# Seven products of a weight pair in another order: the high weights of two products, then their low ones

## The chip, the cores and the metric

The kernel runs on one core of a Trainium2 chip. The metric is device time in microseconds (us) of one execution, the median of several runs.

## The reference

One layer of a streaming encoder over 512 tokens and 2048 channels, all in float32. A normalised input is multiplied by one wide projection matrix, whose outputs are queries, keys, values and gates of two mixers (sparse attention and a retention recurrence) and two merge gates. The mixers' outputs are projected back, gated, added and sent through `w_o`; a gated side input and a last normalisation follow. Cut to the products, which are nearly all of the work:

```
h = rmsnorm(x)
proj = h @ w_in                      # 2048 x 13392: aq ak av az iq ik iw rq rk rv rz ga gb
a_out = dsa_mixer(aq, ak, av, iq, ik, iw) * silu(az)
b_out = retention_mixer(rope(rq), rope(rk), rv) * silu(rz)
merged = sigmoid(ga) * (a_out @ w_a_out) + sigmoid(gb) * (b_out @ w_b_out)
r = x + merged @ w_o
y = r + (p @ w_ple) * sigmoid(r @ w_ple_gate)
return rmsnorm(y) * final_gain
```

## The kernel before

**Two parts a number.** A float32 operand is split into a high part, rounded to what TensorE's fast float32 form keeps, and a low part, the rest. A product is high by high, high by low and low by high. For weights the high part `wh` is an ACT copy (L137) and the low part `wl` is a DVE subtraction (L142), each of a block of 8 tiles of 128x128, called a unit.

**Pairs.** 48 times, two column blocks of 128 outputs each are computed together by `gemm_pair` (L214): 40 pairs of `w_in` (24 in the retention and gate section, then 4, 8 and 4) and 8 of `w_o`. A pair replaces eight half-sized block products by seven, on sums and differences of the weight blocks and of the activation blocks (named in `PRODUCTS`). So a pair has seven units of weights and seven products, numbered 0 to 6. Each product accumulates into one of four PSUM banks: `banks = (v, p, q, r, p, v, p)`. An activation tile holds its high part in columns 0 to 255 and its low part in columns 256 to 511. So a product is 8 matmuls of the high weights over all 512 columns and 8 of the low weights over the first 256: 112 matmuls a pair, all on L259.

**The order within a pair.** Product by product, 0 to 6; the high weights come first and the low ones second, except in products 4 and 6, where the low weights come first. In this text 0h is the group of eight matmuls with the high weights of product 0, 0l that with its low ones. The order is 0h 0l 1h 1l 2h 2l 3h 3l 4l 4h 5h 5l 6l 6h. After products 0, 1, 4 and 6, ACT copies a bank to SBUF (`pv`, `e1`, `e2`, `e3`, L225); after products 2, 5 and 6, DVE combines banks and copies to outputs (`out`, L227 to L230, then the caller's `done`, such as L887). In the first pair of `w_o` (`late`) the products 0 and 1 run on the first seven tiles and then on the eighth, because the last activations come late.

**Requests.** The emission of instructions is one Python program; the engines run apart, each in the order of its own instructions, held by semaphores. `split_to(n)` (L122) emits the splits of all units below n: at once the ACT copy (L137), and one step later the function `rest`, which holds DVE's subtraction (L142). A step is two matmuls (L262). Where the unit's raw weights are then to become a sum, `rest` also adds another raw tile on DVE (L144) or starts a DMA on the POOL queue that adds a block from HBM into the tile (L105). At the start of product n `split_to` asks for the unit three further (`AHEAD`), and `load_to` (L107) emits the loads on the SP queue for units eight further (L116). There are three buffers each for `wh` and `wl` (`W_BUFS`), and seven for raw tiles (`RAW_BUFS`): a split waits until the matmuls three units back have read the buffer, and a load waits until a raw tile is free. Within a pair, unit 5's ACT copy reads the tile that the DVE addition behind unit 4 (L144) has made.

**Other work in between.** `step` also emits what is due from `later` and from background lists: retention (L743), the top-k rounds and the bias tables. In the retention section the two gate pairs behind each of the eight heads' pairs carry extra matmuls and DVE work.

Of the kernel before, what the change touches and what calls it, by code (L numbers as in the profile page):

```python
# [35 lines left out]
def block_kernel(tc, xT, pT, posb, posq, w_in, w_v, w_ik, w_a, w_b, w_o, w_ple, w_gate,  # L36
                 w_gt, w_pt, fgb, tab, gains, cst, dec, out, out_a, out_b):
    nc = tc.nc
    pe, dve, act, pool, sp = nc.tensor, nc.vector, nc.scalar, nc.gpsimd, nc.sync

    with contextlib.ExitStack() as ctx:
# [10 lines left out]
        def U(name, dt=F32):  # L52
            return up.tile([128, L], dt, name=name, tag="u")
# [4 lines left out]
        def P(name):  # L58
            return pp.tile([128, L], F32, name=name, tag="p")
# [10 lines left out]
        loaded = {}  # L70
# [29 lines left out]
        def view(t, nk, cols):  # L100
            return t.rearrange("p a c -> p (a c)")[:, 0:nk * cols].rearrange("p (a c) -> p a c", c=cols)

        def add_block(r, b):
            src, k0 = b
            pool.dma_start(out=raw_tiles[r], in_=src[:, k0:k0 + 8, :], accum_op=OP.add)  # L105

        def load_to(n):  # L107
            need = max((u[0] for u in units[:n]), default=-1) + 1
            while state["raw"] < need:
                i = state["raw"]  # L110
                src, k0, nk, cols, plus = raws[i]
                if nk * cols <= L and i < 4:
                    t = U("wraw4").rearrange("p (a c) -> p a c", c=128)
                else:
                    t = wp.tile([128, 8, 128], F32, name="wraw", tag="wraw", bufs=RAW_BUFS)
                sp.dma_start(view(t, nk, cols), src[:, k0:k0 + nk, :])  # L116
                raw_tiles[i] = t
                if plus is not None:
                    add_block(i, plus)
                state["raw"] += 1  # L120

        def split_to(n):  # L122
            while state["split"] < min(n, len(units)):
                i = state["split"]
                load_to(i + 1)
                r, plus, nk, cols = units[i]
                if r in unfinished:
                    unfinished[r]()
                raw = view(raw_tiles[r], nk, cols)
                if i in in_raws:  # L130
                    t = wp.tile([128, 2, 512], F32R, name="whl", tag="wraw", bufs=RAW_BUFS)
                    h, l = t[:, 0:1], t[:, 1:2]
                elif nk * cols == L:
                    h, l = (U(n, F32R).rearrange("p (a c) -> p a c", c=cols) for n in ("wh4", "wl4"))
                else:
                    h, l = (view(wp.tile([128, 8, 128], F32R, name=n, tag=n), nk, cols) for n in ("wh", "wl"))
                act.activation(h, raw, AF.Copy)  # L137

                def rest(r=r, plus=plus, l=l, raw=raw, h=h):
                    if unfinished.pop(r, None) is None:  # L140
                        return
                    dve.tensor_sub(l, raw, h.bitcast(F32))  # L142
                    if isinstance(plus, int):
                        dve.tensor_add(raw, raw, view(raw_tiles[plus], nk, cols))  # L144
                    elif plus is not None:
                        add_block(r, plus)

                unfinished[r] = rest
                later(1, rest)
                loaded[i] = (h, l)  # L150
                state["split"] += 1

# [6 lines left out]
        def later(n, f):  # L159
            if n <= 0:  # L160
                return f()
            tick[1] += 1
            heapq.heappush(soon, (tick[0] + n, tick[1], f))

        def step():
            tick[0] += 1
            while soon and soon[0][0] <= tick[0]:
                heapq.heappop(soon)[2]()
            f = todo.popleft() if todo else None
            if f is not None:  # L170
                f()
            elif bg and tick[0] % state["rate"] == 0:
                bg.popleft()()
# [31 lines left out]
        ALL = slice(0, L)  # L205
# [4 lines left out]

        LO, HI = slice(0, 256), slice(256, 512)
        PRODUCTS = ("s3", "a11", "a12", "s4", "s2", "a22", "s1")

        def gemm_pair(ids, X, done, late=False):  # L214

            p, v, q, r = (P("ps_" + n) for n in ("p", "v", "q", "r"))  # L220
            E = {}

            def copy(n, src):
                E[n] = U(n)
                act.activation(E[n], src, AF.Copy)  # L225

            def out(f, x, y, i, c):  # L227
                t = U("e_t")
                f(t, x, y)
                done(t[:, LO], t[:, HI], i, c)  # L230

            def last():
                copy("e3", p)
                out(dve.tensor_sub, p, E["pv"], 1, HI)
                out(dve.tensor_add, r, E["e3"], 1, LO)

            after = {
                0: lambda: copy("pv", v),
                1: lambda: copy("e1", p),
                2: lambda: out(dve.tensor_sub, q, E["e1"], 0, LO),  # L240
                4: lambda: copy("e2", p),
                5: lambda: out(dve.tensor_sub, v, E["e2"], 0, HI),
                6: last,
            }
            banks = (v, p, q, r, p, v, p)
            runs = [(n, range(8), True) for n in range(7)]
            if late:
                runs[0:2] = [(n, range(7), False) for n in (0, 1)] + [(n, (7,), True) for n in (0, 1)]
            count = 0
            for n, ks, end in runs:  # L250
                i, o = ids[n], banks[n]
                if ks[0] == 0:
                    split_to(i + AHEAD - (late and n == 1))
                    load_to(i + AHEAD + LOADS)
                parts = (1, 0) if n in (4, 6) else (0, 1)
                for part in parts:
                    w, c = loaded[i][part], (ALL, LO)[part]
                    for k in ks:
                        pe.matmul(o[:, c], w[:, k], X[PRODUCTS[n]][k][:, c], start=(n < 4 and part == 0 and k == 0),  # L259
                                  stop=(part == parts[1] and k == 7), skip_group_check=True)  # L260
                        count += 1
                        if count % 2 == 0:  # L262
                            step()
                if end and n in after:
                    after[n]()

        def combos(lo, hi, name, keep=None):


            X = {n: [None] * 8 for n in PRODUCTS}  # L270
            T = {}
# [138 lines left out]

        x_split(0)
        split_to(1)
        step()
        x_split(1)
# [254 lines left out]
        hd = dp.tile([56, 128, L], F32, name="hd")  # L669
        x_at = {(n, k): hd[8 * i + k] for i, n in enumerate(PRODUCTS) for k in range(8)}  # L670
        xn = {}
# [10 lines left out]
        _, h_step = combos(lambda k: xn[k], lambda k: xn[k + 8], "h", lambda n, k: x_at[n, k])  # L682
# [168 lines left out]

        Xh = {n: [None] * 8 for n in PRODUCTS}
        x_wanted = collections.deque((n, k) for n in PRODUCTS for k in range(8))

# [25 lines left out]
        def gate_pair(ids, finish):  # L880
            t = B("go")
            outs = [t[:, 0:512], t[:, 512:1024]]
            have = [0, 0]

            def done(c0, c1, i, q):
                o = outs[i]
                dve.tensor_add(o[:, q], c0, c1)  # L887
                have[i] += 1
                if have[i] == 2:
                    later(1, lambda: finish(i, o))  # L890

            gemm_pair(ids, Xh, done)
# [196 lines left out]
        for m in PAIRED:  # L1089
            t = B("sm")  # L1090
            s, o = t[:, 0:512], t[:, 512:1024]
# [17 lines left out]
        for m in range(8):  # L1109
# [9 lines left out]
            def done(c0, c1, i, q, xc=xc):  # L1119
                dve.tensor_add(xc[i][:, q], xc[i][:, q], c0)  # L1120
                dve.tensor_add(xc[i][:, q], xc[i][:, q], c1)
# [14 lines left out]
        for m in range(MF):  # L1136
            i = u_p[m // 4][0]
# [5 lines left out]
            for k in range(2):  # L1143
                a, b = pparts[k]
                w = 2 * (m % 4) + k
# [129 lines left out]
        for i in range(2):  # L1275
            c = (slice(0, 384), slice(384, 512))[i]
# [16 lines left out]
        for q in range(MF // 4):  # L1293
            o = U("yo")
# [6 lines left out]
            o = o.rearrange("p (a c) -> p a c", a=4)  # L1301
# [9 lines left out]
AHEAD = 3  # L1311
LOADS = 5
# [101 lines left out]
```

## Time and profile before

| what | value |
|---|---|
| median of 3 runs | 1686.25 us (1686.04 to 1686.39) |
| profiled execution | 1686.46 us |
| its span, first to last instruction | 1684.7 us |
| granted TensorE clock | 0.998 |
| DVE busy | 1275.3 us (76%) |
| ACT busy | 863.0 us (51%) |
| DMA moved | 355.85 MB, mean 211 GB/s |

The share of busy time on TensorE (PE) counts overlapping matmuls once, and a matmul's end is modelled. So the time that a matmul takes of PE is read here from start to start: in the timeline, consecutive matmuls of one group are one row, and a row's start minus the start before it is what the group before took. In the timeline's rows the first number is the start in us from the span's start, the second the time to the end of the last instruction, then engine, line, operation, output and inputs, shapes and count; a bracket gives idle time before it and what ended it.

### The profile page before, as it was taken

Reading aid. Unit: us, or ns where it says so; the run is one execution under the profiler, and the core shown is the slowest. Engines: PE = TensorE matmul, PEld = TensorE weight load, DVE = VectorE, ACT = ScalarE, POOL = GpSimd, SP = SyncE. Lnnn points to the kernel's source line nnn. Section 1 sums busy time; section 2 is a strip of 40 time slices with the busy share of each in tenths; the row PEclk is TensorE's granted clock in tenths of the full one; section 3 lists DMA queues with packets and bytes.
Section 4 is the critical chain, followed back from the end, with each engine's and each line's share of the span. In section 5 each row is a group of like instructions: output and inputs, shape, how many; then the busy total and the mean of one; then the engine's idle time right before and its main releaser. Section 6 shows DMA issues by size and latency. Waiting matters only on the chain.

```text
span 1684.7 us, 24747 instructions
## 1 busy us (share of the span) xinstructions
PE 1672.4 (99%) x9208; PEld 1451.1 (86%) x9208; DVE 1275.3 (76%) x2020; ACT 863.0 (51%) x1278; POOL 214.8 (13%) x216
## 2 busy tenths in 40 slices
PE   9999999999999999999999999999999999999997
PEld 7988888888888888888888888888888888888897
DVE  7797888987878878877876876787768877864453
ACT  7465423555555555555554555566644444463342
POOL 2100000111111111111331111100000111112222
PEclk9999999999999999999999999999999999999999
DMA  7438989788788788788988889898566788733222
GB/s 288 126 107 310 374 298 327 182 229 220 183 219 213 200 215 212 198 213 215 250 237 214 217 206 233 246 368 278 177 200 189 193 229 214 204 116 100 88 63 100
DMA packets 135369, 355.85 MB, mean 211 GB/s; under 512 B 14801, under 2 KB 26961, under 8 KB 135249
## 3 DMA queue, kind: packets, MB, share of 16 engines
q1 hardware_dynamic: 102496, 256.20, 44.3%
q0 software_dynamic: 21376, 77.60, 25.5%
q10 hardware_dynamic: 11376, 20.47, 3.3%
q8 instruction: 72, 1.18, 0.3%
q14 instruction: 49, 0.39, 0.1%
HBM read 301.26 MB, written 52.95 MB: 210 GB/s over the span
## 4 chain that ended last, share of the span: by engine, by line
PE 94%; DVE 2%; ACT 1%; DMA 1%; issue 1%; POOL 0%; SPq 0%; POOLq 0%; ACTq 0%; DVEq 0%
PE ps_p L259 23%; PE ps_v L259 16%; PE ps_r L259 8%; PE ps_q L259 8%; PE ps_vn L726 3%; PE ps_vn L727 3%; PE ps_vn L728 3%; PE ps_w L198 3%; PE ps_w L197 3%; PE ps_w L199 3%; PE ps_pg L199 3%; PE ps_pg L197 3%; PE ps_pg L198 3%; PE ps_iq L197 1%; PE ps_iq L199 1%; PE ps_iq L198 1%
## 5 line engine op out<-in xcount | busy, mean ns | idle before, releaser
L142 DVE TENSOR_TENSOR wl<-wraw,wh 128x1024 fp32r<-128x1024 f32 (+2 forms) x459 | 562.1, 1232 | 201.7 <-ACT wh L137 198.4
L137 ACT ACTIVATE wh<-wraw 128x1024 fp32r<-128x1024 f32 (+2 forms) x459 | 474.1, 1042 | 283.5 <-DVE wraw L144 129.3
L105 POOL DMA_DIRECT2D wraw<-w_in x120 | 106.3, 960 | 837.6 <-DVE wl L142 264.3
L225 ACT ACTIVATE e<-ps_p 128x512 f32<-128x512 f32 x144 | 86.1, 598 | 158.6 <-PE ps_p L259 151.5
L259 PE MATMUL ps_p<-hs,wh 128*128 128x512 f32 x640 | 161.3, 394 | 0.0
L259 PEld LDWEIGHTS ps_p<-hs,wh 128*128 128x128 f32 x640 | 114.9, 189 | 21.2 <-issue 0.7
L726 PE MATMUL ps_vn<-wh,hh 128*128 128x512 f32 x256 | 99.8, 390 | 0.0
L727 PE MATMUL ps_vn<-wl,hh 128*128 128x512 f32 x256 | 99.7, 390 | 0.0
L728 PE MATMUL ps_vn<-wh,hl 128*128 128x512 f32 x256 | 99.7, 389 | 0.0
L259 PE MATMUL ps_p<-hs,wl 128*128 128x256 f32 x640 | 92.0, 284 | 0.7 <-DVE wl L142 0.7
L259 PEld LDWEIGHTS ps_p<-hs,wl 128*128 128x128 f32 x640 | 83.0, 192 | 1.4 <-DVE wl L142 0.9
L259 PE MATMUL ps_r<-hs,wh 128*128 128x512 f32 x320 | 82.2, 395 | 0.0
L259 PE MATMUL ps_v<-ha,wh 128*128 128x512 f32 x320 | 80.6, 393 | 0.0
L259 PE MATMUL ps_p<-ha,wh 128*128 128x512 f32 x320 | 80.4, 393 | 0.0
L259 PE MATMUL ps_q<-ha,wh 128*128 128x512 f32 x320 | 80.1, 392 | 0.0
L259 PE MATMUL ps_v<-hs,wh 128*128 128x512 f32 x320 | 79.6, 390 | 0.1
L199 PE MATMUL ps_pg<-rh,wl 128*128 128x512 f32 x192 | 74.8, 390 | 0.0
L197 PE MATMUL ps_pg<-rh,wh 128*128 128x512 f32 x192 | 74.7, 389 | 0.0
L198 PE MATMUL ps_pg<-rl,wh 128*128 128x512 f32 x192 | 74.7, 389 | 0.0
L887 DVE TENSOR_TENSOR go<-e_t 128x256 f32<-128x256 f32 x160 | 68.1, 425 | 5.6
L259 PEld LDWEIGHTS ps_v<-hs,wh 128*128 128x128 f32 x320 | 59.8, 188 | 13.2 <-ACT wh L137 0.5
L259 PEld LDWEIGHTS ps_v<-ha,wh 128*128 128x128 f32 x320 | 59.3, 188 | 12.5 <-issue 0.5
(361 smaller groups left out, 3499.4 us busy)
## 6 DMA issues: line engine op xcount, KB each, us to landing
wraw<-w_in SPq DMA_DIRECT2D x172, 512.0 KB, 5.5
wraw<-w_in POOLq DMA_DIRECT2D x120, 512.0 KB, 8.4
wraw<-w_v SPq DMA_DIRECT2D x32, 512.0 KB, 5.0
wraw<-w_o SPq DMA_DIRECT2D x32, 512.0 KB, 5.1
wraw<-w_o POOLq DMA_DIRECT2D x24, 512.0 KB, 6.7
wraw<-w_gate SPq DMA_DIRECT2D x24, 512.0 KB, 4.1
hd<-hs SPq DMA_DIRECT2D x32, 256.0 KB, 5.2
hs<-hd SPq DMA_DIRECT2D x32, 256.0 KB, 5.4
```

The lines of the kernel that those rows point to most:

```text
L105: pool.dma_start(out=raw_tiles[r], in_=src[:, k0:k0 + 8, :], accum_op=OP.add)
L137: act.activation(h, raw, AF.Copy)
L142: dve.tensor_sub(l, raw, h.bitcast(F32))
L197: pe.matmul(o, h[:, k, w], a, start=(s == order[0]), stop=False)
L198: pe.matmul(o, h[:, k, w], b, start=False, stop=False)
L199: pe.matmul(o, l[:, k, w], a, start=False, stop=(s == order[-1]))
L225: act.activation(E[n], src, AF.Copy)
L259: pe.matmul(o[:, c], w[:, k], X[PRODUCTS[n]][k][:, c], start=(n < 4 and part == 0 and k == 0), stop=(part == parts[1] and k == 7), skip_gr ...
L726: pe.matmul(pss[t], a[:, tok(t)], h[:, k], start=(s == 0), stop=False)
L727: pe.matmul(pss[t], a[:, tok(t)], l[:, k], start=False, stop=False)
L728: pe.matmul(pss[t], b[:, tok(t)], h[:, k], start=False, stop=(s == KT - 1))
L887: dve.tensor_add(o[:, q], c0, c1)
```

## The change

The order of the fourteen groups of a pair becomes 0h 1h 0l 1l 2h 3h 2l 3l 4l 4h 5h 5l 6l 6h: the first four products in twos. From 4l on nothing is moved. In the late pair the first four groups run on seven tiles and then on the eighth.

The requests are moved with it. `SPLIT_AT` gives, by place in the new order, up to which unit is asked for. Unit 3 is now asked for at 0l (place 2), before the copy `pv` rather than behind it, and its DVE subtraction is emitted five steps later instead of one, so that it stands behind 0l, whose buffer of low weights it overwrites. Unit 5 is asked for at 3l (place 7), behind 2l, instead of at 3h. In the late pair unit 3 is asked for at 1l instead. All other units are asked for after as many matmuls as before. Loads are asked for at every second place. SP's order of instructions is the same as before. DVE's combination after product 2 stands behind 2l, now one group later.

```diff
-        def split_to(n):
+        def split_to(n, lag=1):
...
-                later(1, rest)
+                later(lag, rest)
...
+        RUNS = [(n, part) for part, ns in enumerate(((0, 1), (0, 1), (2, 3), (2, 3, 4), (4, 5), (5, 6), (6,)))
+                for n in ns]
+        RUNS = [(n, part % 2) for n, part in RUNS]
+
+        SPLIT_AT = {0: 3, 2: 4, 3: 4, 4: 5, 7: 6, 8: 7, 10: 8, 12: 9}
+        LOAD_AT = (0, 2, 4, 6, 8, 10, 12)
...
-            runs = [(n, range(8), True) for n in range(7)]
+            runs = [(n, part, range(8)) for n, part in RUNS]
             if late:
-                runs[0:2] = [(n, range(7), False) for n in (0, 1)] + [(n, (7,), True) for n in (0, 1)]
+                runs[0:4] = [(n, part, ks) for ks in (range(7), (7,)) for n, part, _ in runs[0:4]]
+            ended = [0] * 7
             count = 0
-            for n, ks, end in runs:
+            for at, (n, part, ks) in enumerate(runs):
+                at = max(at - 4, 0) if late else at
                 i, o = ids[n], banks[n]
-                if ks[0] == 0:
-                    split_to(i + AHEAD - (late and n == 1))
-                    load_to(i + AHEAD + LOADS)
-                parts = (1, 0) if n in (4, 6) else (0, 1)
-                for part in parts:
-                    w, c = loaded[i][part], (ALL, LO)[part]
-                    for k in ks:
-                        pe.matmul(o[:, c], w[:, k], X[PRODUCTS[n]][k][:, c], start=(n < 4 and part == 0 and k == 0),
-                                  stop=(part == parts[1] and k == 7), skip_group_check=True)
-                        count += 1
-                        if count % 2 == 0:
-                            step()
-                if end and n in after:
+                if at in SPLIT_AT and not (late and at == 2):
+                    split_to(ids[0] + SPLIT_AT[at], 5 if at == 2 else 1)
+                if at in LOAD_AT:
+                    load_to(ids[LOAD_AT.index(at)] + AHEAD + LOADS)
+                w, c = loaded[i][part], (ALL, LO)[part]
+                first = ended[n] == 0
+                for k in ks:
+                    ended[n] += 1
+                    pe.matmul(o[:, c], w[:, k], X[PRODUCTS[n]][k][:, c], start=(n < 4 and first and k == 0),
+                              stop=(ended[n] == 16), skip_group_check=True)
+                    count += 1
+                    if count % 2 == 0:
+                        step()
+                if ended[n] == 16 and n in after:
                     after[n]()
```

## The prediction

> **What bounds the kernel now.** I read the page first: span, busy times, and the chain that ended last.
>
> ```profile
> span 1684.7 us, 24747 instructions
> ...
> PE 1672.4 (99%) x9208; PEld 1451.1 (86%) x9208; DVE 1275.3 (76%) x2020; ACT 863.0 (51%) x1278; POOL 214.8 (13%) x216
> ...
> PE 94%; DVE 2%; ACT 1%; DMA 1%; issue 1%; POOL 0%; SPq 0%; POOLq 0%; ACTq 0%; DVEq 0%
> ```
>
> PE is never free: 99% busy, 94% of the chain. DVE and ACT matter only where a split comes after the matmul that wants it. Next, PE's own waits, the whole of what the waits view has for L259:
>
> ```profile
> PE ps_p L259 <- DVE wl L142: 0.7, 1, 0.7
> ```
>
> One wait over 0.15 us in 5376 matmuls. So no waiting worth the name is there to be removed; what the change can give must come out of the matmuls' own pace. For that I read the timeline of one undisturbed pair (the second of the four az pairs), PE alone:
>
> ```profile
> 1046.78 1.98 PE L259 MATMUL ps_v<-hs,wh 128*128 128x512 f32 x8
> 1048.59 1.12 PE L259 MATMUL ps_v<-hs,wl 128*128 128x256 f32 x8
> 1049.54 2.00 PE L259 MATMUL ps_p<-ha,wh 128*128 128x512 f32 x8
> 1051.38 1.12 PE L259 MATMUL ps_p<-ha,wl 128*128 128x256 f32 x8
> 1052.34 2.00 PE L259 MATMUL ps_q<-ha,wh 128*128 128x512 f32 x8
> 1054.18 1.11 PE L259 MATMUL ps_q<-ha,wl 128*128 128x256 f32 x8
> 1055.13 2.00 PE L259 MATMUL ps_r<-hs,wh 128*128 128x512 f32 x8
> 1056.97 1.11 PE L259 MATMUL ps_r<-hs,wl 128*128 128x256 f32 x8
> 1057.92 1.12 PE L259 MATMUL ps_p<-hs,wl 128*128 128x256 f32 x8
> 1058.88 2.00 PE L259 MATMUL ps_p<-hs,wh 128*128 128x512 f32 x8
> 1060.72 1.98 PE L259 MATMUL ps_v<-ha,wh 128*128 128x512 f32 x8
> 1062.54 1.11 PE L259 MATMUL ps_v<-ha,wl 128*128 128x256 f32 x8
> 1063.49 1.12 PE L259 MATMUL ps_p<-hs,wl 128*128 128x256 f32 x8
> 1064.45 2.00 PE L259 MATMUL ps_p<-hs,wh 128*128 128x512 f32 x8
> 1066.29 0.39 PE L259 MATMUL ps_v<-hs,wh 128*128 128x512 f32 x1
> ```
>
> Differences of starts give what each group takes. High groups (wh) behind a low one: 1h 1051.38 - 1049.54 = 1.84, and 2h, 3h, 4h, 6h also 1.84. High groups behind a high one: 0h 1.81, 5h 1.82, so 1.815. Low groups (wl) behind a high one: 0.95, 0.96, 0.95, 0.95, 0.95, mean 0.952; behind a low one (4l, 6l) 0.96. A step from low to high thus costs a high group 0.025 us, and a step from high to low saves a low group 0.008: a net 0.017 us for each time the pair goes down and up again. The pair takes 19.51.
>
> **The change part by part.**
>
> *The order of the groups.* Before, a pair steps from low to high at 1h, 2h, 3h, 4h and 6h. After, 1h stands behind 0h and 3h behind 2h; 1l stands behind 0l and 3l behind 2l. Nothing is added or removed: 112 matmuls either way. So two high groups fall from 1.84 to 1.815 and two low ones rise from 0.952 to 0.96: 2 x 0.025 - 2 x 0.008 = 0.034 us a pair, in 48 pairs 1.6 us. Rounding of the starts leaves the 1.6 open by some 0.3 either way. Runs of sixteen are in the rows above (6h and the next 0h, 4h 5h; 3l 4l, 5l 6l); the new runs of twenty-four (6h 0h 1h; 2l 3l 4l) are not, and I take them at the rates of the second eight. Bounds: nothing (if the 0.025 were the price of something that stays), and 48 x 2 x 0.025 = 2.4 if the low groups did not rise. I take the 1.6.
>
> The Trainium skill ("TensorE: Matmul & The Clock Gate", Back-to-back issue gap) has another rule: a warm matmul takes its column count divided by 2.4 GHz plus about 2.5 ns of its own, so eight would take 1.73 us at 512 columns and 0.87 at 256, whatever stands before them. By it the order of groups saves nothing; the rows above (1.84 against 1.815) do not agree, as far as one pair shows.
>
> *The requests.* What must be in time after the change? From the group times, the new order has, from the start of the pair: 1h at 1.81, 0l 3.63, 1l 4.58, 2h 5.54, 3h 7.38, 2l 9.20, 3l 10.15, 4l 11.11, 4h 12.07, 5h 13.91, 5l 15.72, 6l 16.68. From 4l on that is 0.03 earlier than before. In the same pair, ACT and then DVE:
>
> ```profile
> 1050.89 0.60 ACT L225 ACTIVATE pv<-ps_v 128x512 f32<-128x512 f32 x1 [0.40 <-ACT go L896]
> 1051.39 1.05 ACT L137 ACTIVATE wh<-wraw 128x1024 fp32r<-128x1024 f32 x1
> 1052.54 0.60 ACT L225 ACTIVATE e<-ps_p 128x512 f32<-128x512 f32 x1
> 1053.03 1.06 ACT L137 ACTIVATE wh<-wraw 128x1024 fp32r<-128x1024 f32 x1
> 1056.69 2.01 ACT L137 ACTIVATE wh<-wraw 128x1024 fp32r<-128x1024 f32 x2 [2.61 <-DVE wraw L144]
> ```
> ```profile
> 1052.47 1.23 DVE L142 TENSOR_TENSOR wl<-wraw,wh 128x1024 fp32r<-128x1024 f32 x1 [1.51 <-ACT wh L137]
> 1054.12 1.22 DVE L142 TENSOR_TENSOR wl<-wraw,wh 128x1024 fp32r<-128x1024 f32 x1 [0.42 <-ACT wh L137]
> 1055.38 1.22 DVE L144 TENSOR_TENSOR wraw<-wraw 128x1024 f32<-128x1024 f32 x1
> 1056.52 0.68 DVE L229 TENSOR_TENSOR e_t<-ps_q,e 128x512 f32<-128x512 f32 x1
> 1057.24 0.43 DVE L887 TENSOR_TENSOR go<-e_t 128x256 f32<-128x256 f32 x1
> 1057.79 2.36 DVE L142 TENSOR_TENSOR wl<-wraw,wh 128x1024 fp32r<-128x1024 f32 x2
> ```
>
> Unit 3's high copy (1051.39, that is 4.61 into the pair) stood behind `pv`, which stood behind the caller's `go`. Now it goes ahead of `pv`, into its place behind `go` (1050.89, that is 4.11), and ends at 5.2. It is wanted at 7.38, which was 8.35: 2.2 us to spare, where there were 2.7. Its low part starts at 5.2 instead of 5.69 and is wanted at 10.15: more to spare. `pv` now needs 0l, over at 4.58, and runs about 5.2 to 5.8; `e1` 5.76 as before; unit 4's copy 6.25 as before, and with it DVE's L142 and L144, over at 1056.60 (9.82). So unit 4 pays nothing. Then DVE's combination of bank q (L229, L887) must wait for 2l: over at 10.15 plus about 0.2, by which `e1` follows 1l. It runs 10.35 to 11.5 instead of 9.74 to 10.89, and behind it in DVE's queue the low parts of units 5 and 6 slip by 0.6, from 11.01 to 13.37 to about 11.6 to 14.0. They are wanted at 15.72 and 16.68: 2.9 and 2.7 us to spare. Loads wait for those subtractions to free raw tiles, so they start 0.6 later; a unit's load leads its split by most of a pair, and that hides it. The first weights of the next pair keep their times, but its 1h is wanted 0.95 earlier.
>
> So an undisturbed pair stalls nowhere. The price falls where a copy was already late, on 3h above all. One pair (the fourth of the qk pairs) shows it:
>
> ```profile
> 928.20 2.11 PE L259 MATMUL ps_v<-hs,wh 128*128 128x512 f32 x8
> 930.14 1.11 PE L259 MATMUL ps_v<-hs,wl 128*128 128x256 f32 x8
> ```
> ```profile
> 934.61 0.33 ACTq L924 DMA_DIRECT2D kd<-go  x1
> 934.98 0.60 ACT L225 ACTIVATE pv<-ps_v 128x512 f32<-128x512 f32 x1 [1.70 <-DVE go L887]
> 935.47 1.05 ACT L137 ACTIVATE wh<-wraw 128x1024 fp32r<-128x1024 f32 x1
> ```
>
> Its 0h took 1.94, 0.13 over. 3h will be wanted at 928.20 + 0.13 + 7.38 = 935.71. The copy moves up into the place of `pv`, 934.98 to 936.03: a stall of about 0.3. In the pairs of the retention section similar queues stand; the one PE wait of 0.7 above is a low part at the end of a DVE queue that the change does not shorten, so it stays. I take 0.3 for all such places, between nothing (they all have cover) and 2 (six more pairs with 0.3).
>
> *Sum.* 1.6 - 0.3 = 1.3 us. Own time of the profiled execution: 1686.46, of which 1684.7 is span and 1.76 lies around it and stays. 1686.46 - 1.3 = 1685.2; the median of the runs stands 0.2 lower, so 1684.9.
>
> **The rivals.**
>
> *The order saves nothing:* the 0.025 belongs to certain products or banks (0h and 5h, both in v) and not to what stands before. For it: both quick groups write bank v. Against: low groups show the opposite sign by neighbour. Then only the stall is left: 1686.25 + 0.3 = 1686.6.
>
> *Faster:* the freed order also lets the one wait of 0.7 go and no new stall comes: 1684.9 - 0.7 - 0.3 = 1683.9, and 2.4 instead of 1.6 gives 1683.1. Nothing in the rows leads further down.
>
> *Slower:* three low groups in a row (2l 3l 4l) use up three units of low weights in 2.87 us, where DVE makes one in 1.22, with L144 and retention work between. The place is 4l in the gate pairs behind a head. One of them:
>
> ```profile
> 564.34 1.22 DVE L142 TENSOR_TENSOR wl<-wraw,wh 128x1024 fp32r<-128x1024 f32 x1
> ```
> ```profile
> 567.03 1.12 PE L259 MATMUL ps_p<-hs,wl 128*128 128x256 f32 x8
> ```
>
> The low part is done at 565.56, 1.47 before 4l. If the later subtraction of unit 3 (five steps) or the later q combination makes DVE's queue slip by more than that in these pairs, PE stalls in each. A slip of 2.0 costs 0.5 in sixteen pairs, 8 us: 1692.9. It decides from 1.47 on. Against: the slip that I find is 0.6, and behind L144, not ahead of it.
>
> **How the numbers follow.** Forecast (1684.2 to 1686.2, by the rounding and the stalls between 0 and 2): 0.70. Order saves nothing (1686.3 to 1686.9): 0.11. Faster yet (1683.1 to 1684.2): 0.07. Slower: 0.12, mostly near 1690 and above. The range 1683.1 to 1687.5 leaves out the slower case alone. A measurement of this kernel tells about 0.2% from no change, here 3.4 us. Faster than 1682.9 needs more than any row gives: 0.05, taken half from the forecast and half from the faster case. Slower than 1689.6: 0.12. Between them: 0.83.
>
> **What would show it.** In the same pair of the changed kernel: group times 1.81 to 1.82 at 1h and 3h, 0.96 at 1l and 3l, a pair of 19.48 instead of 19.51 (1.84 at 1h and 3h speaks for the first rival); unit 3's copy ahead of `pv`; the q combination about 10.35 into the pair and the next low parts 0.6 later. PE's waits on L259: still the one of 0.7 or so, and 0.3 before 3h in the pair near 928. I am wrong if PE waits for L142 or L137 in many pairs, above all before 3h or 4l behind a head, or if runs of twenty-four matmuls keep another pace.

## The result and the profile after

The changed kernel takes 1684.16 us (median of 22 runs, 1683.21 to 1684.77), the kernel before 1686.01 (22 runs beside them, 1684.93 to 1690.12). The ratio is 0.9988 (95% interval 0.9982 to 0.9993): 1.85 us faster, with 1.2 to 3.0 inside the interval. The forecast was a gain of 1.3 us, to 1684.9. The profiled execution took 1684.08 us.

First the page of the changed kernel: span, busy times and the chain that ended last.

```profile
span 1682.3 us, 24757 instructions
...
PE 1669.6 (99%) x9208; PEld 1450.9 (86%) x9208; DVE 1275.8 (76%) x2020; ACT 864.8 (51%) x1278; POOL 216.4 (13%) x216
...
PE 95%; DVE 2%; ACT 1%; issue 1%; DMA 0%; POOL 0%; SPq 0%; POOLq 0%; DVEq 0%; ACTq 0%
```

PE is still the bound. The span is 2.4 us shorter, and PE's busy time fell by 2.8 with the same 9208 matmuls: the same work at a quicker pace, for the most part (0.6 us of it is waiting that the views do not list, as the second profiles below show). PE's waits view of the changed kernel has one line for the matmuls of the pairs, which now stand on L267:

```profile
PE ps_r L267 <- ACT wh L137: 0.4, 1, 0.4
```

The one wait of 0.7 on a low part is gone; one of 0.4 on a high part has come. Both lie in the first gate pair of the retention section: before it was 4l that waited, now it is 3h (and behind it 3l for 0.14, below what the view lists):

```profile
306.54 2.12 PE L267 MATMUL ps_r<-hs,wh 128*128 128x512 f32 x8 [0.40 <-ACT wh L137]
```

From start to start that pair takes 24.35 us where it took 24.36, so the waits cost about the same. The pace itself is read in the same undisturbed pair as before, the second of the az pairs, PE alone:

```profile
1044.68 1.98 PE L267 MATMUL ps_v<-hs,wh 128*128 128x512 f32 x8
1046.49 1.98 PE L267 MATMUL ps_p<-ha,wh 128*128 128x512 f32 x8
1048.31 1.11 PE L267 MATMUL ps_v<-hs,wl 128*128 128x256 f32 x8
1049.26 1.12 PE L267 MATMUL ps_p<-ha,wl 128*128 128x256 f32 x8
1050.22 2.00 PE L267 MATMUL ps_q<-ha,wh 128*128 128x512 f32 x8
1052.06 1.98 PE L267 MATMUL ps_r<-hs,wh 128*128 128x512 f32 x8
1053.87 1.11 PE L267 MATMUL ps_q<-ha,wl 128*128 128x256 f32 x8
1054.82 1.12 PE L267 MATMUL ps_r<-hs,wl 128*128 128x256 f32 x8
1055.78 1.12 PE L267 MATMUL ps_p<-hs,wl 128*128 128x256 f32 x8
1056.74 2.00 PE L267 MATMUL ps_p<-hs,wh 128*128 128x512 f32 x8
1058.59 1.98 PE L267 MATMUL ps_v<-ha,wh 128*128 128x512 f32 x8
1060.40 1.12 PE L267 MATMUL ps_v<-ha,wl 128*128 128x256 f32 x8
1061.35 1.12 PE L267 MATMUL ps_p<-hs,wl 128*128 128x256 f32 x8
1062.31 2.00 PE L267 MATMUL ps_p<-hs,wh 128*128 128x512 f32 x8
1064.15 0.62 PE L267 MATMUL ps_v<-hs,wh 128*128 128x512 f32 x2
```

Read the differences of the starts. 1h takes 1048.31 - 1046.49 = 1.82 and 3h 1053.87 - 1052.06 = 1.81, where both took 1.84. 1l takes 0.96 and 3l 0.96, where they took 0.95. The pair takes 19.47 instead of 19.51. This is what the prediction wanted to see for its first step.

In the same pair, ACT and then DVE show the requests:

```profile
1047.75 0.64 ACT L904 ACTIVATE go<-go 128x512 f32<-128x512 f32 x1 [1.33 <-DVE go L895]
...
1048.84 1.06 ACT L137 ACTIVATE wh<-wraw 128x1024 fp32r<-128x1024 f32 x1 [0.46 <-ACT go L904]
1049.81 0.58 ACT L230 ACTIVATE pv<-ps_v 128x512 f32<-128x512 f32 x1
1050.42 0.60 ACT L230 ACTIVATE e<-ps_p 128x512 f32<-128x512 f32 x1
```
```profile
1055.02 0.69 DVE L234 TENSOR_TENSOR e_t<-ps_q,e 128x512 f32<-128x512 f32 x1 [0.54 <-PE ps_q L267]
1055.75 0.42 DVE L895 TENSOR_TENSOR go<-e_t 128x256 f32<-128x256 f32 x1
1056.09 2.35 DVE L142 TENSOR_TENSOR wl<-wraw,wh 128x1024 fp32r<-128x1024 f32 x2
```

Unit 3's copy runs ahead of `pv`, 4.16 into the pair (1048.84 - 1044.68) and over at 5.22, which leaves 2.2 us until 3h at 7.38. The combination of bank q starts at 10.34 and waits for PE, as forecast; the low parts of units 5 and 6 start behind it at 11.41. None of this reaches PE.

Where did the 2.35 us between the two profiled spans come from? Start to start, pair by pair: 1.83 from the other 44 pairs, 0.59 from the third and fourth of the qk pairs, 0.01 from the first gate pair, -0.10 from the late pair (the single matmuls on the eighth tile), and 0.02 before, between and behind the pairs.

### The profile page after: what moved, and what is told of

It reads as the page before. It is cut to its first block, busy times and chain, and to the rows that moved or that the text cites. A ratio compares the mean times of both kernels' runs of the same rounds, so it can differ in the third digit from the quotient of the medians.

```text
span 1682.3 us, 24757 instructions
## 1 busy us (share of the span) xinstructions
PE 1669.6 (99%) x9208; PEld 1450.9 (86%) x9208; DVE 1275.8 (76%) x2020; ACT 864.8 (51%) x1278; POOL 216.4 (13%) x216
## 4 chain that ended last, share of the span: by engine, by line
PE 95%; DVE 2%; ACT 1%; issue 1%; DMA 0%; POOL 0%; SPq 0%; POOLq 0%; DVEq 0%; ACTq 0%
PE ps_p L267 24%; PE ps_v L267 16%; PE ps_r L267 8%; PE ps_q L267 8%; PE ps_vn L734 3%; PE ps_vn L735 3%; PE ps_vn L736 3%; PE ps_w L198 3%; PE ps_w L197 3%; PE ps_w L199 3%; PE ps_pg L199 3%; PE ps_pg L197 3%; PE ps_pg L198 3%; PE ps_iq L197 1%; PE ps_iq L199 1%; PE ps_iq L198 1%
## 5 line engine op out<-in xcount | busy, mean ns | idle before, releaser
L267 PE MATMUL ps_p<-hs,wh 128*128 128x512 f32 x640 | 161.3, 394 | 0.0
L267 PEld LDWEIGHTS ps_p<-hs,wh 128*128 128x128 f32 x640 | 114.9, 189 | 21.2 <-issue 0.7
L267 PE MATMUL ps_p<-hs,wl 128*128 128x256 f32 x640 | 92.0, 284 | 0.0
L267 PEld LDWEIGHTS ps_p<-hs,wl 128*128 128x128 f32 x640 | 83.0, 192 | 0.5 <-issue 0.4
L267 PE MATMUL ps_v<-ha,wh 128*128 128x512 f32 x320 | 80.6, 393 | 0.0
L267 PE MATMUL ps_q<-ha,wh 128*128 128x512 f32 x320 | 80.1, 392 | 0.0
L267 PE MATMUL ps_r<-hs,wh 128*128 128x512 f32 x320 | 79.2, 389 | 0.4 <-ACT wh L137 0.4
L267 PE MATMUL ps_v<-hs,wh 128*128 128x512 f32 x320 | 79.5, 390 | 0.0
L267 PE MATMUL ps_p<-ha,wh 128*128 128x512 f32 x320 | 79.2, 390 | 0.0
L267 PEld LDWEIGHTS ps_r<-hs,wh 128*128 128x128 f32 x320 | 60.0, 188 | 13.3 <-ACT wh L137 0.8
L267 PEld LDWEIGHTS ps_p<-ha,wh 128*128 128x128 f32 x320 | 60.0, 188 | 12.9 <-issue 0.4
```

## The experiments

In this section a **step** is a place where a group of low matmuls is followed by one of high ones. The kernel before has five a pair, the changed kernel three. "Undisturbed pair" is the median, start to start, of the same sixteen pairs in each trace, which have no other matmuls in them; but for the kernel in threes they agree within 3 ns in every kernel.

### Is it the order, and is the price one per step?

Four kernels are the changed one with nothing but the list of groups replaced, so that the requests stay as changed:

```diff
-        RUNS = [(n, part % 2) for n, part in RUNS]
+        RUNS = [(int(g[0]), "hl".index(g[1])) for g in "0h 1h 0l 1l 2h 2l 3h 3l 4l 4h 5h 5l 6l 6h".split()]
```

That is the first of them; the others have "0h 0l 1h 1l 2h 3h 2l 3l ..." (second half alone), the order of before, and high weights first in all seven products.

> The order 0h 1h 0l 1l 2h 2l 3h 3l, then as before; requests as in the changed kernel. One of the two steps from low to high is gone. Theory (a step costs what stands before the group): an undisturbed pair takes 19.49 us, half way between 19.51 and 19.47, the kernel 0.9 us less than before (half of the 1.8 of the whole change), and only 1h is at 1.815, 3h at 1.84. Rival (the requests, not the order, give the gain): nearly the whole 1.8 us, pairs that wait less, undisturbed pairs the same 19.51. Rival (bank or product): 1h stays at 1.84.

> The order 0h 0l 1h 1l 2h 3h 2l 3l, then as before; requests as in the changed kernel. Theory: 19.49 us a pair, 0.9 us less than before, 3h at 1.815 and 1h at 1.84, so that both halves add up to the whole. Rival (requests): nearly the whole 1.8 us in this one too. Rival (bank or product): 3h stays at 1.84.

> All fourteen groups in the order of before, requests by the table of the changed kernel (unit 5 asked for one group later, unit 3's low part five steps later). Theory: an undisturbed pair 19.51 us and the kernel within 0.4 us of before. Rival (requests give the gain): 1 to 2 us faster than before at 19.51 us a pair.

> High weights first in all seven products, also in 4 and 6, requests by the table of the changed kernel: a pair goes from low to high seven times instead of five. Theory: two steps more at 0.018 us, an undisturbed pair 19.55 us, the kernel 1.7 us slower than before, all high groups at 1.84 and all low ones at 0.952. Rival (bank or product, or requests): 19.51 us and no difference.

| kernel | steps | undisturbed pair, us | time, us | ratio to before (95%) |
|---|---|---|---|---|
| before | 5 | 19.513 | 1686.01 | |
| changed | 3 | 19.473 | 1684.16 | 0.9988 (0.9982 to 0.9993) |
| first half alone | 4 | 19.493 | 1685.80 | 0.9994 (0.9985 to 1.0003) |
| second half alone | 4 | 19.493 | 1685.82 | 0.9998 (0.9989 to 1.0007) |
| old order, new requests | 5 | 19.513 | 1686.00 | 1.0000 (0.9991 to 1.0009) |
| high first everywhere | 7 | 19.553 | 1687.20 | 1.0007 (0.9998 to 1.0016) |

The pair goes up by 20 ns a step, wherever in the pair the step stands. The rival that tied the pace to certain banks or products falls: both halves give the same, and with high weights first in products 4 and 6 too, every group behind a low one is slow. The requests by themselves give nothing to the pair: old order with new requests is 19.513 again. The times of the runs alone could not have shown this, since the intervals of neighbouring kernels overlap; 16 pairs of a trace can. The last four kernels ran 11 times each, beside 33 runs of the kernel before with a median of 1686.21, to which their ratios belong. Their medians lie 0.4, 0.4 and 0.2 us below it and 1.0 above it, where 0.9, 0.9, nothing and 1.7 were expected; the intervals hold both.

### What is a step the price of?

Three theories were open. The matmuls over 256 columns may be so short that something ahead of the array runs empty, and the first wide ones pay (A). Any change of width may cost (B). Or the price may be of going over from one kind of weights to the other. The width of the low matmuls was changed, with nothing else:

```diff
-                w, c = loaded[i][part], (ALL, LO)[part]
+                w, c = loaded[i][part], (ALL, slice(0, 320))[part]
```

> The changed kernel with its low-weight matmuls over 320 columns instead of 256: it adds the low-weight product for 64 more tokens. A low interval is then about 147 ns by the line through 120 at 256 and 227 at 512 columns: 56 x 27 ns = 1.5 us more a pair. Theory A (the step is the price of the first high matmuls after matmuls so short that something ahead of the array runs empty): the high group behind a low one falls from 1.84 to 1.815. Theory B (every change of width costs the same): it stays at 1.84.

> The changed kernel with its low-weight matmuls over 192 columns instead of 256: it leaves out the low-weight product for 64 of the 256 tokens. If the 120 ns of a low matmul go by its columns (the line through 120 at 256 and 227 at 512), it takes about 93 ns and a pair is 1.5 us shorter; if 120 ns is a floor set by the weights, it stays at 120 and the pair at 19.47. Theory A expects the high group behind a low one to take at least 1.84, more if shorter matmuls empty more of what runs ahead; theory B 1.84.

> The changed kernel with its low-weight matmuls over 448 columns: it adds the low-weight product for 192 more tokens. By the line through 120, 147 and 227 a low interval is 200 ns and a pair without steps 56 x 426.7 ns = 23.89 us. If a change of width costs a fixed price: the first five high matmuls behind a low one take 25 ns more than five later ones, as at 256 (23 at 320), and the pair 23.95. If the price grows with the difference of the widths (64 columns here, 256 in the changed kernel): some 6 ns, and the pair 23.91.

> The changed kernel with its low-weight matmuls over all 512 columns: it adds the low-weight product for the 256 tokens that the other kernels leave out. Rows of 512 alone keep 226.7 ns. If the step is the price of a change of width, nothing changes width any more: the first high matmuls behind low ones take 227 like all others and an undisturbed pair 112 x 226.7 = 25.39 us. If it is the price of going over to other weights (from wl to wh), the first five still take 233, 236, 228, 232, 231 and the pair some 25.45.

The timeline of the same pair on PE, first with low matmuls over all 512 columns, then over 320, 448 and 192; the row with `ps_q<-ha,wh`, behind a low group, is 2h:

```profile
1263.84 1.98 PE L267 MATMUL ps_v<-hs,wh 128*128 128x512 f32 x8
...
1269.28 1.98 PE L267 MATMUL ps_p<-ha,wl 128*128 128x512 f32 x8
1271.10 1.98 PE L267 MATMUL ps_q<-ha,wh 128*128 128x512 f32 x8
1272.91 1.98 PE L267 MATMUL ps_r<-hs,wh 128*128 128x512 f32 x8
1274.72 1.98 PE L267 MATMUL ps_q<-ha,wl 128*128 128x512 f32 x8
...
1289.23 1.07 PE L267 MATMUL ps_v<-hs,wh 128*128 128x512 f32 x4
```
```profile
1104.00 1.33 PE L267 MATMUL ps_p<-ha,wl 128*128 128x320 f32 x8
1105.17 2.00 PE L267 MATMUL ps_q<-ha,wh 128*128 128x512 f32 x8
1107.01 1.98 PE L267 MATMUL ps_r<-hs,wh 128*128 128x512 f32 x8
1108.83 1.33 PE L267 MATMUL ps_q<-ha,wl 128*128 128x320 f32 x8
```
```profile
1220.07 1.78 PE L267 MATMUL ps_p<-ha,wl 128*128 128x448 f32 x8
1221.69 2.00 PE L267 MATMUL ps_q<-ha,wh 128*128 128x512 f32 x8
1223.53 1.98 PE L267 MATMUL ps_r<-hs,wh 128*128 128x512 f32 x8
1225.34 1.78 PE L267 MATMUL ps_q<-ha,wl 128*128 128x448 f32 x8
```
```profile
1036.98 1.05 PE L267 MATMUL ps_p<-ha,wl 128*128 128x192 f32 x8
1037.87 2.01 PE L267 MATMUL ps_q<-ha,wh 128*128 128x512 f32 x8
1039.72 1.98 PE L267 MATMUL ps_r<-hs,wh 128*128 128x512 f32 x8
1041.53 1.03 PE L267 MATMUL ps_q<-ha,wl 128*128 128x192 f32 x8
```

With one width, 2h takes 1.81 behind low weights, and the pair 25.39 = 112 x 226.7 ns to the last digit: **going over to other weights is free, the step is the price of a change of width** (the columns that a matmul reads and writes). With 320 columns 2h still takes 1.84, so A as stated falls. With 448 columns, only 64 fewer than the high ones, it takes 1.84 again: the price does not grow with the difference of widths. The single intervals between starts (medians, ns, of the groups of sixteen) say how it is paid:

| low columns | first intervals of a high group behind a low one | steady | first intervals of a low group behind a high one | steady |
|---|---|---|---|---|
| 192 | 253 232 231 | 227 | 86 113 113 | 112 (109 117 109 112 in turn) |
| 256 | 233 236 228 232 231 | 227 | 113 119 | 120 |
| 320 | 231 236 228 232 231 | 227 | 143 145 | 147 |
| 448 | 235 229 233 230 | 227 | 199 | 202.7 (199 207 203 202 203 in turn) |
| 512 | 227 | 227 | 227 | 227 |

The steady pace of one width is kept from the sixth wide matmul on at the latest. Taken off the pair (56 times 226.67 and 56 times the low pace, from pairs of 20.967, 19.473, 24.107 and 18.987 us), what is left for each of three steps is 20 ns at 320 and at 256 columns, 20 to 23 at 448 (where the low pace is known to 0.1 ns only) and 13 at 192. Two expectations were off: at 448 columns a low interval is 202.7 ns and not 200, so the pair took 24.11 and not 23.95, and at 192 columns it is 112 and not 93. So at 192 columns something other than the columns sets the pace; the runs do not show what, nor why the step is cheaper there. Why a change of width costs time at all stays open too: theory A falls in the form in which it was stated, and nothing here looks inside the engine.

### Is the split request of unit 3 needed?

```diff
-                    split_to(ids[0] + SPLIT_AT[at], 5 if at == 2 else 1)
+                    split_to(ids[0] + SPLIT_AT[at], 1)
```

> The changed kernel with the low part of unit 3 requested one step after its high part instead of five. The theory (DVE has 3 us of cover here): undisturbed pair 19.47, time within 0.4 us of the changed kernel, no wait over 0.5 on the matmul line that the changed kernel lacks. The rival (the split request is what keeps the order free of stalls): DVE's subtraction stands at the head of its queue waiting for the copy, what is behind it comes later, and PE waits for L142 in the retention pairs: over 1 us more in all.

It took 1684.18 us (10 runs; ratio to before 0.9988, 0.9979 to 0.9997), the undisturbed pair 19.473. On the matmul line it has the same wait of 0.4 on a high part and one of 0.3 on a low part in the same gate pair. The theory holds: the five steps of lag are worth nothing that a measurement here can tell. One pair differs: the fourth qk pair takes 19.69 here, with 3h at 1.95.

### One step fewer

If a step costs 20 ns, groups in threes should save another one a pair, as far as the weights are ready. In every pair but the late one:

```diff
-            runs = [(n, part, range(8)) for n, part in RUNS]
+            runs = [(n, part, range(8)) for n, part in (RUNS if late else THREES)]
```

with `THREES` the order 0h 1h 2h 0l 1l 2l 3h 4h 5h 3l 4l 5l 6l 6h and requests of its own by a like table.

> Order 0h 1h 2h, 0l 1l 2l, 3h 4h 5h, 3l 4l 5l 6l, 6h in every pair but the late one: two steps from low to high a pair instead of three. The theory (each step costs 0.018 to 0.02 us): an undisturbed pair of 19.45 us instead of 19.47, 47 x 0.018 = 0.85 us less than the changed kernel where nothing waits, so about 1683.3. The rival (no cover left): with three high groups in a row the copy of unit 5 is ready only 0.5 us ahead of 5h and the low part of unit 6 0.5 ahead of 6l, so that the retention pairs, whose queues run later than that, make PE wait for L137 or L142: more than 0.85 us of waits on the matmul line, 1685 to 1695.

It took 1704.83 us (5 runs, 1701.22 to 1709.91; ratio to before 1.0110, 1.0096 to 1.0125): the rival is right, and its price was set too low. PE's waits on the matmul line of this kernel:

```profile
PE ps_v L273 <- ACT wh L137: 10.4, 14, 2.2
...
PE ps_p L273 <- ACT e L232: 2.9, 1, 2.9
PE ps_p L273 <- DVE wl L142: 0.2, 1, 0.2
```

Fourteen times 5h (the only high group into bank v besides 0h) stands before a copy that is not there, all in or just behind the retention section; once, in the third qk pair, 6l waits for the copy that empties its bank. The profiled span is 19.0 us longer than the changed kernel's; the fifteen pairs with these stalls have 18.4 us more. Not all of that is waiting. The longest of these waits, of 2.93, is followed by 3.4 us in which the granted clock is 0.50, the only such stretch in this trace but for its end. 6h falls into it and takes 3.04 us instead of 1.84:

```profile
942.44 3.20 PE L273 MATMUL ps_p<-hs,wh 128*128 128x512 f32 x8
945.48 0.86 PE L273 MATMUL ps_v<-hs,wh 128*128 128x512 f32 x3
```

With 6l before it (1.42 instead of 0.95) that is 1.7 us more in this pair. The five runs' mean granted clocks, 0.998 in the fastest (1701.22) down to 0.995 in the slowest (1709.91), suggest that some have more such stretches; only one has a trace.

An undisturbed pair took 19.45 where 5h had its copy 0.22 us ahead (the second az pair), as the price per step says, and 19.47 in most: there the copy is over 0.16 ahead, and 5h's first matmuls lose the 20 ns again (intervals of 228 to 233 ns) without a wait that the view lists.

So the order that is cheapest by pace here is dearest by cover. Threes in the sixteen undisturbed pairs alone would save at most 16 x 0.02 = 0.3 us, less than a run can tell; it was not tried.

### What does one profile scatter?

Both kernels were profiled once more.

> The kernel before, a second profile. Undisturbed pairs 19.51 us as in the first. What differs between the two profiles is scatter, and no difference of that size between other single profiles is to be explained: I expect the third and fourth of the qk pairs (19.77 each in the first) to differ by 0.3 to 1 us, and the span by as much.

> The changed kernel, a second profile. Undisturbed pairs 19.47 us again. If the stall of 0.3 that I had forecast for the fourth qk pair is there in some executions and not in others, that pair takes 19.5 to 20 us here, and 19.47 if the change itself removed it.

Before took 1686.38 us, changed 1683.95. The undisturbed pairs are 19.513 and 19.473 again. The third and fourth qk pairs take 20.15 and 19.79 in the kernel before (19.77 each in the first profile), and 19.47 and 19.47 in the changed one, both times. So in both profiles of each the two kernels differ here: 0.6 and 1.0 us of their difference sit in these two pairs.

The chain behind it can be followed in POOL and ACT. The first two fences are the kernel before, the next two the changed one: POOL's DMA that adds a block into a raw tile, then the two ACT copies that wait for it.

```profile
918.32 0.88 POOL L105 DMA_DIRECT2D wraw<-w_in  x1 [8.94 <-issue]
```
```profile
927.09 2.01 ACT L137 ACTIVATE wh<-wraw 128x1024 fp32r<-128x1024 f32 x2 [3.91 <-DMA wraw<-w_in]
```
```profile
915.29 0.88 POOL L105 DMA_DIRECT2D wraw<-w_in  x1 [7.25 <-issue]
```
```profile
923.87 2.01 ACT L137 ACTIVATE wh<-wraw 128x1024 fp32r<-128x1024 f32 x2 [2.07 <-DMA wraw<-w_in]
```

The pair starts at 908.43 before and at 907.09 after. Before, POOL's add goes out 9.89 into it, just behind the landing of the tile's load (9.27), and the copies start at 18.66: the first is over about 0.2 after the next pair wants it. The waits view of the first profile misses this: PE sat idle for only 0.09 before that next pair and yet lost 0.26, because the end of a matmul of 512 columns is modelled 0.16 behind the place where the next one can start (it lasts 389 ns, the next starts after 227). After, the load lands at 7.57, the add goes out at 8.20 and the copies start at 16.78, in time. In the kernel with 192 columns, whose pairs are half a microsecond shorter, the load landed at 11.40 and PE waited 3.5 us for the same copy:

```profile
PE ps_v L267 <- ACT wh L137: 3.5, 1, 3.5
```

The second profiles agree: the load landed at 9.25 before and at 7.48 after. What sets the landing of that one load stays open. It is one of seven that stand on SP's queue behind four writes to a scratch tensor, among POOL's and ACT's transfers; it was issued at -1.87 in the changed kernel and at -0.57 before, but at -1.87 too with the first half alone, where it landed at 10.20. The time of issue alone does not settle it.

## Why the prediction was right, and where it was not

**The order of the groups: right in mechanism, mis-sized by a sixth.** 1h, 3h, 1l, 3l and the pair moved as forecast. The prediction had 0.017 us a step out of starts rounded to 0.01; the pairs give 0.020. Over 44 pairs that is 44 x 2 x 0.020 = 1.76, and they measured 1.83 in all (some retention pairs gain a little more, one behind a head goes from 24.21 to 24.13); the sum had 1.6 for 48. The new runs of twenty-four keep the pace, as assumed: 24 high matmuls show 227 ns from the sixth on, 24 low ones 120 from the third.

The Trainium skill ("TensorE: Matmul & The Clock Gate", Back-to-back issue gap) gave the rule from which the prediction drew that order would save nothing: columns divided by 2.4 GHz plus about 2.5 ns. The section itself calls this the gap of an isolated matmul; for a stream of weight loads and matmuls, as these pairs are, it has a sustained 131 ns at 512 columns, which the prediction left out. The measurements decide against both. Steady intervals are 226.7, 146.7 and 120 ns at 512, 320 and 256 columns, that is columns divided by 2.4 GHz plus 13.3 ns, and each change of width adds 20 ns that no such formula has. What the prediction drew from the rule holds in one case: with one width (the kernel with 512 columns everywhere) it does not matter what stands before a matmul.

**The requests: right.** Nothing in an undisturbed pair stalls; the starts of the copy, of `pv` and of the q combination came within 0.07 of the forecast (low parts of units 5 and 6 0.2 earlier).

**The stall of 0.3 at 3h in the fourth qk pair: wrong, and of the other sign.** The step took that pair's late start as given and asked what a moved copy would do in it. But the lateness was the end of a chain from the pair before, a load that landed late, and in the changed kernel that load lands 1.7 us sooner. The two pairs gained 0.6 us in the first profiles and 1.0 in the second, instead of losing 0.3. The mechanism itself (3h wanted earlier than its copy) is real. It came in the first gate pair, with 0.40. It also comes in the fourth qk pair where the load still lands late: with the second half alone it landed at 8.95, the fourth qk pair started late, and 3h, whose copy stands behind `pv` in that order, waits 0.68 there:

```profile
935.95 2.11 PE L265 MATMUL ps_r<-hs,wh 128*128 128x512 f32 x8 [0.68 <-ACT wh L137]
```

With the changed order and the requests one step apart the load landed at 8.74, and 2h and 3h lost 0.2 in that pair, nearly the stall that was forecast.

**The one wait of 0.7 stays: wrong in form, right in sum.** The wait moves with the requests and the order, within the same pair: with the old order and the new requests it is 0.5 on 3l, in the changed kernel 0.40 on 3h and 0.14 on 3l, with the requests one step apart 0.4 on 3h and 0.3 on 4l. The pair takes 24.35 to 24.37 in all of them.

**The late pair** was not in the sum; it lost 0.1.

The sum was thus 1.6 - 0.3 = 1.3, where the profiles have 1.8 + 0.6 - 0.1 = 2.3 and the medians 1.85. The interval of the medians, 1.2 to 3.0, holds both sums; only the pairs of the traces tell them apart. The measured 1684.16 lies just below the forecast's own 1684.2 to 1686.2, in the part of the range that was given to "faster yet" with a chance of 0.07.

**The rivals.** "The order saves nothing" fell with the kernels of 3, 4, 5 and 7 steps. "Faster yet" (1683.9) lies closer to the measured time than the forecast, for half of the right reason: a stall less and a dearer step, but not the stall that it named. "Slower", 4l behind three low groups in the gate pairs, did not come. In the gate pair near 554 the second of these two low parts is unit 4's, over at 564.95, and 4l starts 1.42 later:

```profile
562.60 2.35 DVE L142 TENSOR_TENSOR wl<-wraw,wh 128x1024 fp32r<-128x1024 f32 x2
```
```profile
566.37 1.12 PE L267 MATMUL ps_p<-hs,wl 128*128 128x256 f32 x8
```

It had been 1.47: DVE's queue slips behind unit 4's low part, as argued, and not ahead of it. The kernel in threes shows that the family of this rival is the one to fear: the cover of 5h runs out in thirteen of the 24 retention pairs, and an order that was to save 0.85 us costs 19.

## What to carry to other kernels

Where an engine is 99% busy, compare the same group of instructions behind different neighbours, start to start: a price per change of shape shows there, and multiplied by its count it is most of the gain to be had there. Sort like shapes together only as far as the operands' cover reaches: here the next sorting step cost 19 us where the two before it had given 1.8. And before pricing a stall that a change adds to a late place, follow that lateness back to its origin, since the change may move the origin.

## What the hardware showed that was not expected

- A change of the width of the moving operand costs about 20 ns net per down-and-up, nearly the same between 512 and 448, 320 or 256 columns (13 between 512 and 192); it is paid by the first four or five wide matmuls (228 to 236 ns instead of 227), and the first one or two narrow ones give a little back (113 and 119 instead of 120). A change from one weight block to another without a change of width costs nothing.
- Steady intervals follow one line at 256, 320 and 512 columns, 0.417 ns a column ((226.7 - 120) / 256) plus 13.3 ns, but not at 448 (202.7 instead of 200, in a period of five) nor at 192 (112 instead of 93, in a period of four).
- A load of 512 KB among other transfers landed between 7.5 and 11.4 us into one and the same pair in the kernels with low matmuls of 256 and 192 columns, while two profiles of one kernel agree within 0.1; PE waited up to 3.5 us for what hung on it.
- Behind a wait of PE of 2.93 us (the kernel in threes) the granted clock was 0.50 for 3.4 us; behind one of 3.47 (192 columns) it stayed at 1.00. What decides this the runs do not show.
